# Trainium2, one core: the first pass of an encoder trunk with c from columns, chunk scales on ScalarE and the first query strip in another bank

## The chip, the core and the metric

The kernel runs on one core of one Trainium2 chip. The core has TensorE (PE in the profile, its weight loads PEld), VectorE (DVE), ScalarE (ACT), GpSimd (POOL) and SyncE (SP), which issues nearly all DMA transfers. Each engine works through its own instruction queue in order; semaphores let one wait for another. The metric is the device time of one execution in microseconds; less is better.

## What is computed

Two layers on 1024 tokens of width 1024 in float32, each with an RMS norm, a shift, scale and gate from a conditioning vector c, a token mixer, a SiLU gate and an output projection. Layer 0 is differential attention, layer 1 latent attention. The change touches only the start of layer 0:

```python
def _modulation(c, ada_w, ada_b):
    mod = jax.nn.silu(c) @ ada_w + ada_b
    shift, scale, gate = jnp.split(mod[:, None, :], 3, axis=-1)
    return shift, scale, gate
...
    for i in range(DEPTH):
        shift, scale, gate = _modulation(c, ada_w[i], ada_b[i])
        h = _rmsnorm(x, norm_g[i]) * (1.0 + scale) + shift
...
    proj = h @ w_in
    q, k, v, z = jnp.split(proj, [DA_WIDTH, 2 * DA_WIDTH, 3 * DA_WIDTH], axis=-1)
```

## The kernel before

All matrix products split a float32 operand into a high and a low part (names ending in h and l, or hi and lo) and add three products: high by high, high by low, low by high (`mm3`, lines 173 to 175). The high part is made by a cast on ACT, the low part by a subtraction on POOL or DVE.

**Start.** SP loads the small vectors (`vec`), the row of c (`crow`), four tiles of x (128 tokens x 1024), then the modulation weights. Line 561 issues warm-up matmuls on a tile of ones, 8 before the spread of c and 9 behind it (`WARM`). Lines 600 and 601 form silu(c) times two on one partition (the half stands in the dot's scale), and line 605 spreads it over all 128 partitions with a one-row matmul into `cb`, a PSUM tile of two banks. Tokens are scaled by their inverse RMS in two pieces: the first 256 columns (`X_CUT`) on ACT (lines 618 and 621), the other 768 on DVE (line 624, `x_rest`).

**First pass, tokens 0 to 511** (the loop from line 661 on). It runs over eight chunks k of 128 features. For each, SP loads two modulation weight tiles (`ada`, 512 KB each, four buffers) and a tile of value weights (`wvr`, 256 KB, two buffers). `mod_pair` does two dots of the ada tiles with cb on DVE (line 439) for shift and scale, and line 447 turns the scale into (1 + scale) times the norm's gain, one column, on DVE. `h_chunk` transposes four blocks of x on PE (line 487) and applies scale and shift on ACT twice, once rounded (h0h, line 492) and once in full (line 494); POOL subtracts (h0l, line 497). Then PE adds the chunk to four value accumulators (`vacc`) and one of a key strip (`kacc`): 15 matmuls of 512 columns on lines 712 to 718. Between the chunks DVE reduces the angles of the rotary tables (lines 580 to 595), ACT takes their sines (lines 633 to 636) and copies cb to SBUF (`c2`, line 637), for the modulation of layer 1.

**Behind it.** PE computes the first query strip (`qacc`, 24 matmuls) in a bank of the tag acc, which it shares with the value accumulators. ACT and DVE empty the accumulators into `v_hl` (lines 377 and 378), square and scale the other four x tiles (lines 530 to 532 and 732 to 733), and the **second half**, tokens 512 to 1023, goes through the same chunks, every second one transposed into the first bank of cb (tile `trc`). Four dots for layer 1 (`MODS_K`, from `mods_g`) stand between its chunks. Strips for key, query and gate follow, then the values of the other heads and the attention.

**What sets the order.** Instructions are issued by priority as their operands become ready in a schedule made at build time; `tc.issue_after(x)` keeps an instruction behind x. On the chip every queue then runs in that fixed order. A buffer is loaded again once its last reader is done, and `bank("acc", ...)` deals out five banks in turn.

Of the kernel before, what the change touches and what calls it, by code (L numbers as in the profile page):

```python
# [21 lines left out]
P = 128  # L22
# [10 lines left out]
      ("ada_bsc1", KT), ("subln_g", 1), ("q_a_norm_g", 3), ("kv_a_norm_g", 2), ("inv", 1), ("ada_bg0", KT), ("ada_bg1", KT)]  # L33
# [30 lines left out]
WARM = (8, 9)  # L64
# [17 lines left out]
def trunk(ctx: ExitStack, tc: tile.TileContext, A, out):  # L82
# [292 lines left out]
    def store_v(l, sp, acc, tt, fh, tag="vst", bufs=None):  # L375
        v = sp.tile([P, 2, HF], F32R, name="v_hl", tag=tag, bufs=bufs or VB[l])
        store_v.act = S.copy(v[:, 0, :], acc).ins
        V.tensor_sub(v[:, 1, :], acc, f32v(v[:, 0, :]))
# [62 lines left out]
    def mod_pair(l, j, ws, c_):  # L441

        g, bsh, bsc, a_, b_ = mods[l]
        js = slice(j, j + 1)
        mod_dot(ws[0], bsh[:, js], b_[:, js], c_)
        mod_dot(ws[1], bsc[:, js], a_[:, js], c_)
        return V.scalar_tensor_tensor(out=a_[:, js], in0=a_[:, js], scalar=1.0, in1=g[:, js], op0=ALU.add, op1=ALU.mult).ins
# [30 lines left out]
    def h_chunk(l, xn4, k, dst, hp, sub=G, wide=False, act=False, f32=None):  # L478

        _, _, _, a_, b_ = mods[l]  # L480
        if wide:
            tr = bank("cb", "trc", [P, D])[:, :HF].rearrange("p (j q) -> p j q", j=4)
        else:
            tr = bank("tr", "trh", [P, 4, P])
        for j in range(len(xn4)):
            nk = KT // len(xn4[j])
            PE.transpose(tr[:, j, :], xn4[j][k // nk][:, (k % nk) * P : (k % nk + 1) * P], ident)
# [7 lines left out]
        else:  # L495
            V.tensor_scalar(tmp, tr[:, :n, :], ak, bk, op0=ALU.mult, op1=ALU.add)
# [52 lines left out]
    def split_wv(raw, eng=G):  # L549
        h_ = p1b.tile([P, HF], F32R, name="wvh", tag="wv", bufs=16)  # L550
        l_ = p1b.tile([P, HF], F32R, name="wvl", tag="wv", bufs=16)
        S.copy(h_, raw)
# [10 lines left out]
    crow = p1.tile([P, D], F32, name="crow", tag="ada", bufs=ADA_B)  # L563
    th = p1.tile([P, D], F32, name="cth", tag="ada", bufs=ADA_B)
    SP.dma_start(crow[0:1, :], A["c"])
# [44 lines left out]
    y0 = [None] * 4  # L610
# [4 lines left out]
    y_ = inv_rms(ss0[:, 0:3], 3)  # L615
    for j in range(3):
        y0[j] = y_[:, j : j + 1]
        S.mul(xs0[j][0][:, :X_CUT], xs0[j][0][:, :X_CUT], y0[j])
    sq_halves([xs0[3][0][:, :HF], xs0[3][0][:, HF:]], ss0[:, 3:4])
    y0[3] = inv_rms(ss0[:, 3:4], 1)[:, 0:1]  # L620
# [1884 lines left out]
```

## Time and profile before

| | us |
|---|---|
| median of three runs | 1381.55 (1379.77 to 1382.26) |
| the profiled execution, whole | 1382.89 |
| its span | 1380.9 |

| page, share of the span busy | PE | PEld | DVE | ACT | POOL |
|---|---|---|---|---|---|
| | 99% | 83% | 69% | 53% | 51% |

The profile times each instruction of one execution. A row of the timeline has the start and length in us, engine, line, operation and the tiles (out<-in); in square brackets stands how long the engine sat idle before it and what ended that. A row of a window has its limits, then busy time and number of instructions of PE, PEld, DVE, ACT and POOL, the clock granted to TensorE (1.00 is full), the busy share of the DMA engines and the GB/s moved. A group has its count, busy time, mean length in ns, and idle time before it. In this program the span's first 57 us hold the first pass and the query strip.

### The profile page before, as it was taken

What the parts mean: (1) busy time and instruction counts of PE and PEld (TensorE: products, weight loads), DVE (VectorE), ACT (ScalarE), POOL (GpSimd) and SP (SyncE); (2) the same over time, 40 slices, a digit from 0 to 9 for tenths busy, and PEclk for the clock granted to TensorE, in tenths of its full rate; (3) what the DMA queues carried; (4) which work ended last, traced back from release to release, by engine and by line L of the source; (5) the groups of instructions that cost most, each with busy time, mean ns of one, the idle gap of its engine ahead of it and who ended that gap; (6) DMA issues with size and microseconds to landing.
All of it is one profiled execution on the core that took longest, in us unless ns stands there. A gap on an engine that the chain in (4) does not pass through costs nothing.

```text
span 1380.9 us, 20717 instructions
## 1 busy us (share of the span) xinstructions
PE 1361.0 (99%) x7322; PEld 1144.8 (83%) x7322; DVE 949.2 (69%) x1334; ACT 738.3 (53%) x1357; POOL 708.7 (51%) x556
## 2 busy tenths in 40 slices
PE   8999999999999999999999999999999999999997
PEld 6788888888888888887887887788888888888886
DVE  7764788877777767778597987645566555555584
ACT  5633465565655656566648543345454454455554
POOL 4425163647585757565695135532141373834673
PEclk8999999999999999999999999999999999999999
DMA  9867644353444444526654255599343463576373
GB/s 335 275 177 222 211 108 143 113 146 103 156 114 149 135 122 130 153 71 204 210 202 170 60 160 183 161 284 286 115 117 111 111 214 123 190 222 229 118 264 122
DMA packets 149386, 232.06 MB, mean 168 GB/s; under 512 B 20641, under 2 KB 57633, under 8 KB 149282
## 3 DMA queue, kind: packets, MB, share of 16 engines
q1 hardware_dynamic: 149138, 230.48, 53.4%
q8 instruction: 57, 0.93, 0.3%
q14 instruction: 47, 0.39, 0.1%
q10 hardware_dynamic: 144, 0.26, 0.1%
HBM read 144.74 MB, written 61.81 MB: 150 GB/s over the span
## 4 chain that ended last, share of the span: by engine, by line
PE 88%; DVE 4%; DMA 2%; ACT 2%; issue 1%; POOL 1%; SPq 0%; POOLq 0%; DVEq 0%; ACTq 0%
PE s L2109 10%; PE acc L173 9%; PE acc L175 9%; PE acc L174 9%; PE tr L398 8%; PE s L869 8%; PE pv L173 4%; PE pv L174 4%; PE pv L175 4%; PE oy L173 2%; PE oy L174 2%; PE oy L175 2%; PE vps L173 2%; PE vps L174 2%; PE vps L175 2%; PE zacc L175 1%
## 5 line engine op out<-in xcount | busy, mean ns | idle before, releaser
L400 ACT CAST pth<-tr 128x512 fp32r<-128x512 f32 x256 | 150.2, 587 | 279.2 <-PE tr L398 276.3
L401 DVE TENSOR_TENSOR ptl<-tr,pth 128x512 fp32r<-128x512 f32 x256 | 176.3, 689 | 144.6 <-ACT pth L400 143.9
L415 DVE TENSOR_REDUCE nm<-s 128x1 f32<-128x1024 f32 x192 | 234.0, 1219 | 53.7 <-PE s L869 42.9
L219 POOL TENSOR_TENSOR wl<-wraw,wh 128x512 fp32r<-128x512 f32 (+2 forms) x73 | 93.4, 1280 | 264.4 <-ACT wh L218 185.8
L417 ACT ACTIVATE e<-s,nm 128x1024 f32<-128x1024 f32 x128 | 143.7, 1122 | 35.0 <-DVE nm L415 34.4
L398 PE MATMUL tr<-ident,e 128*128 128x128 f32 x1024 | 154.8, 273 | 1.8 <-DVE ptl L401 1.5
L398 PEld LDWEIGHTS tr<-ident,e 128*128 128x128 f32 x1024 | 121.3, 140 | 42.5 <-DVE ptl L401 19.7
L173 PE MATMUL acc<-h0h,wh 128*128 128x512 f32 x360 | 149.5, 415 | 0.0
L173 PE MATMUL pv<-pth,vt 128*128 128x256 f32 x512 | 147.6, 288 | 0.0
L174 PE MATMUL pv<-ptl,vt 128*128 128x256 f32 x512 | 145.4, 284 | 0.0
L175 PE MATMUL pv<-pth,vt 128*128 128x256 f32 x512 | 144.6, 282 | 0.0
L175 PE MATMUL acc<-h0h,wl 128*128 128x512 f32 x360 | 142.0, 394 | 0.0
L174 PE MATMUL acc<-h0l,wh 128*128 128x512 f32 x360 | 141.4, 393 | 0.0
L174 PEld LDWEIGHTS pv<-ptl,vt 128*128 128x128 f32 x512 | 97.5, 190 | 2.5
L1203 POOL TENSOR_TENSOR wol<-wol,woh 128x512 fp32r<-128x512 f32 x56 | 81.9, 1486 | 34.0 <-ACT woh L1202 31.8
L173 PEld LDWEIGHTS pv<-pth,vt 128*128 128x128 f32 x512 | 97.2, 190 | 2.5
L175 PEld LDWEIGHTS pv<-pth,vt 128*128 128x128 f32 x512 | 97.4, 190 | 0.0
L869 PE MATMUL s<-ks,qa 128*128 128x512 f32 x256 | 82.7, 402 | 1.3 <-DVE e L877 1.2
L877 DVE SCALAR_TENSOR_TENSOR e<-s,z,e 128x1024 f32<-128x1024 f32 x64 | 82.2, 1284 | 2.2
L175 PEld LDWEIGHTS acc<-h0h,wl 128*128 128x128 f32 x360 | 67.6, 188 | 14.7
L869 PE MATMUL s<-ks,qb 128*128 128x512 f32 x256 | 79.6, 392 | 0.0
L174 PEld LDWEIGHTS acc<-h0l,wh 128*128 128x128 f32 x360 | 68.2, 189 | 9.2
(433 smaller groups left out, 3416.8 us busy)
## 6 DMA issues: line engine op xcount, KB each, us to landing
ada<-in_ada_ss SPq DMA_DIRECT2D x32, 512.0 KB, 6.1
vS<-v_hl SPq DMA_DIRECT2D x32, 512.0 KB, 5.5
vt<-vS SPq DMA_DIRECT2D x32, 512.0 KB, 4.6
wraw<-in_w_s SPq DMA_DIRECT2D x60, 256.0 KB, 2.8
wol<-tS SPq DMA_DIRECT2D x56, 256.0 KB, 5.3
tS<-ob SPq DMA_DIRECT2D x48, 256.0 KB, 2.2
rp_sw<-rp_raw SPq DMA_DIRECT2D x160, 64.0 KB, 2.0
bc_s<-bc_d SPq DMA_DIRECT2D x34, 256.0 KB, 4.0
```

The lines of the kernel that those rows point to most:

```text
L173: PE.matmul(psum, ah, bh, start=first, stop=False, skip_group_check=skip)
L174: PE.matmul(psum, ah, bl, start=False, stop=False, skip_group_check=skip)
L175: mm3.last = PE.matmul(psum, al, bh, start=False, stop=last, skip_group_check=skip).ins
L219: sub = (V if pair_of else G).tensor_sub(l_[:, :n], raw[:, :n], f32v(h_[:, :n]))
L398: transpose_p.last = PE.transpose(tr[:, j, :], p[:, kt * P : (kt + 1) * P], ident).ins
L400: mk["S"] = S.copy(pth[kh][:, :, dst], tr).ins
L401: mk["V"] = V.tensor_sub(ptl[kh][:, :, dst], tr, f32v(pth[kh][:, :, dst])).ins
L415: mk["V"] = V.reduce_max(nm, s_ps, axis=AX.X, negate=True).ins
L417: mk["S"] = S.activation(e, s_ps, AF.Exp, bias=nm, scale=1.0, accum_out=zs).ins
L869: PE.matmul(s_ps[:, kc * HF : (kc + 1) * HF], src[:, c, ql], KS[h][kc][:, c, :], start=fst, stop=not fst)
L877: combined.append(V.scalar_tensor_tensor(out=e0, in0=e1, scalar=z1[:, 0:1], in1=e0, op0=ALU.mult, op1=ALU.add).ins)
L2109: PE.matmul(s_ps[:, kc * HF : (kc + 1) * HF], lhs, rhs(kc), start=i == 0, stop=i == 4)
```

## The change

- **c from eight columns.** The row `crow` is no longer loaded; c arrives inside `vec` as eight columns of 128. Tanh and product work on 128x8. For each column, DVE multiplies the identity matrix by it (`cd`), and a matmul with ones spreads that block of 128 over all partitions: eight matmuls of 128 columns and 128 rows instead of two of 512 columns and one row. `cd` takes one of the four ada buffers; `crow` and `cth` took two.
- **Chunk scales.** Line 447's product leaves DVE; `mod_scale` does it on ACT just ahead of the chunk.
- **Token scaling.** `x_rest` of tiles 0 and 1 stays on DVE but stands one step later; tiles 2 and 3 go to ACT, behind the casts and the first chunks.
- **TensorE.** 15 instead of 9 warm-up matmuls behind the spread, and three more (`KEEP0`) into kacc behind the first chunk's transposes.
- **Query strip.** `qacc` lies in the second bank of the cb tile (`cbq`); the odd chunks of the second half use its first bank. The copy of cb to `c2` and the split of the query weights move behind the last chunk.
- **Order behind the first pass.** The squares of the second half's x come ahead of emptying the accumulators, its last two tiles are scaled between them, the four dots of layer 1 come behind its last chunk, and some later loads and splits wait for other instructions.

```diff
@@ _W @@
-      ("ada_bsc1", KT), ("subln_g", 1), ("q_a_norm_g", 3), ("kv_a_norm_g", 2), ("inv", 1), ("ada_bg0", KT), ("ada_bg1", KT)]
+      ("ada_bsc1", KT), ("subln_g", 1), ("q_a_norm_g", 3), ("kv_a_norm_g", 2), ("c", KT), ("inv", 1), ("ada_bg0", KT), ("ada_bg1", KT)]
-WARM = (8, 9)
+WARM = (8, 15)
+KEEP0 = 3
@@ strip_half @@
-    def strip_half(w, rhs, half):
+    def strip_half(w, rhs, half, acc=None):
-        acc = bank("acc", "acc")
+        acc = bank("acc", "acc") if acc is None else acc
@@ mod_pair @@
-        g, bsh, bsc, a_, b_ = mods[l]
+        _, bsh, bsc, a_, b_ = mods[l]
         js = slice(j, j + 1)
         mod_dot(ws[0], bsh[:, js], b_[:, js], c_)
-        mod_dot(ws[1], bsc[:, js], a_[:, js], c_)
-        return V.scalar_tensor_tensor(out=a_[:, js], in0=a_[:, js], scalar=1.0, in1=g[:, js], op0=ALU.add, op1=ALU.mult).ins
+        return mod_dot(ws[1], bsc[:, js], a_[:, js], c_).ins
+
+    def mod_scale(l, j):
+
+        g, _, _, a_, _ = mods[l]
+        js = slice(j, j + 1)
+        S.activation(a_[:, js], a_[:, js], AF.Identity, bias=g[:, js], scale=g[:, js])
@@ h_chunk @@
-        if wide:
-            tr = bank("cb", "trc", [P, D])[:, :HF].rearrange("p (j q) -> p j q", j=4)
+        if wide is not None:
+            tr = wide[:, :HF].rearrange("p (j q) -> p j q", j=4)
@@ the spread of c @@
-    crow = p1.tile([P, D], F32, name="crow", tag="ada", bufs=ADA_B)
-    th = p1.tile([P, D], F32, name="cth", tag="ada", bufs=ADA_B)
-    SP.dma_start(crow[0:1, :], A["c"])
+    cd = p1.tile([P, KT, P], F32, name="cd", tag="ada", bufs=ADA_B)
+    th, cs = [sm.tile([P, KT], F32, name="cth") for _ in range(2)]
...
-    c_act = S.activation(th[0:1, :], crow[0:1, :], AF.Tanh, scale=0.5).ins
-    c_last = V.scalar_tensor_tensor(out=crow[0:1, :], in0=th[0:1, :], scalar=1.0, in1=crow[0:1, :], op0=ALU.add, op1=ALU.mult).ins
+    c_act = S.activation(th, part("c"), AF.Tanh, scale=0.5).ins
+    V.scalar_tensor_tensor(out=cs, in0=th, scalar=1.0, in1=part("c"), op0=ALU.add, op1=ALU.mult)
     cb = bank("cb", "cb", [P, D])
-    for f in range(2):
-        fs = slice(f * HF, f * HF + HF)
-        spread = PE.matmul(cb[:, fs], ones[0:1, :], crow[0:1, fs], start=True, stop=True).ins
+    for k in range(KT):
+        c_last = V.tensor_scalar(cd[:, k, :], ident, cs[:, k : k + 1], None, op0=ALU.mult).ins
+        spread = PE.matmul(cb[:, k * P : k * P + P], ones, cd[:, k, :], start=True, stop=True).ins
@@ x_rest @@
-        V.tensor_scalar(xs0[j][0][:, X_CUT:], xs0[j][0][:, X_CUT:], y0[j], None, op0=ALU.mult)
+        rest = xs0[j][0][:, X_CUT:]
+        if j < 2:
+            V.tensor_scalar(rest, rest, y0[j], None, op0=ALU.mult)
+        else:
+            S.mul(rest, rest, y0[j])
@@ sines @@
-                S.copy(c2, cb)
@@ the first pass @@
-        if k < 0:
+        if k == 0:
             with tc.issue_after(m_last):
                 x_rest(0)
                 x_rest(1)
-        if k == 0:
-            with tc.issue_after(m_last):
-                x_rest(2)
-                x_rest(3)
...
-            with tc.issue_after(h_chunk.act):
-                wq0 = split_strip(qraw, None, ada_pair)
-            q_split = load_strip.last
         if 0 <= k < KT:
+            mod_scale(0, k)
             h_chunk(0, xs0, k, h0[k][0], p1, act=True)
+            if k == 0:
+                with tc.issue_after(h_chunk.tr):
+                    for _ in range(KEEP0):
+                        PE.matmul(kacc[:, 0:P], ones, ones, start=True, stop=True)
...
+            if k < 2:
+                with tc.issue_after(h_chunk.act if k else split_wv.act):
+                    x_rest(2 + k)
@@ behind the first pass @@
+    with tc.issue_after(h_chunk.act):
+        S.copy(c2, cb)
+        wq0 = split_strip(qraw, None, ada_pair)
...
-    qacc = strip_half(wq0, h0, 0)
+    cbq = bank("cb", "cbq", [P, D])
+    qacc = strip_half(wq0, h0, 0, cbq[:, HF:])
     q_mm = mm3.last
+    turn += 1
     for tt in range(4):
-        store_v(0, p1b, vacc[tt], tt, 0)
+        with tc.issue_after(x_last):
+            store_v(0, *((p1b, vacc[tt], tt, 0) if tt < 3 else (p1, vacc[tt], tt, 0, "xt", 6)))
+        if tt == 1:
+            yb = inv_rms(ssb, 2)
+            for j in range(2):
+                with tc.issue_after(store_v.v):
+                    V.tensor_scalar(xs1[2 + j][0], xs1[2 + j][0], yb[:, j : j + 1], None, op0=ALU.mult)
+                with tc.issue_after(store_v.act):
+                    S.mul(xs1[2 + j][1], xs1[2 + j][1], yb[:, j : j + 1])
...
-            if 0 < k <= MODS_K:
-                next(mods_g)
-            with tc.issue_after(q_split), tc.issue_after(q_mm):
-                h_last = h_chunk(0, xs1, k, h0[k][1], p1, V if k in HL_V else G, k % 2 == 1)
+            with tc.issue_after(store_v.act), tc.issue_after(q_mm):
+                h_last = h_chunk(0, xs1, k, h0[k][1], p1, V if k in HL_V else G, cbq if k % 2 else None)
+        if k == KT:
+            with tc.issue_after(h_chunk.v):
+                for _ in range(MODS_K):
+                    next(mods_g)
@@ the second value weights @@
-    wv1 = [load_wv(A["w_v0"][k, 1], V) for k in range(WV1)]
+    with tc.issue_after(h_chunk.act):
+        wv1 = [load_wv(A["w_v0"][k, 1], V) for k in range(2)]
```

The order of the instructions on three engines shows where they stand now. A row has line, operation, tile written <- tiles read, and shape; the lines are those of each kernel's own file.

SP, the first loads, in the kernel before (`wvr` and `wraw` are the first value and key weights, `posi` the positions):

```order
L148 DMA vec<-in_vec 128x71
L565 DMA crow<-in_c 1x1024
L523 DMA xt<-in_x 128x1024 x4
L434 DMA ada<-in_ada_ss 128x1024 x2
L543 DMA wvr<-in_w_v 128x512
L197 DMA wraw<-in_w_s 128x512
L543 DMA wvr<-in_w_v 128x512
L434 DMA ada<-in_ada_ss 128x1024
L669 DMA posi<-in_pos 128x256
L434 DMA ada<-in_ada_ss 128x1024 x3
```

SP, the same loads in the changed kernel:

```order
L149 DMA vec<-in_vec 128x79
L530 DMA xt<-in_x 128x1024 x4
L435 DMA ada<-in_ada_ss 128x1024 x2
L550 DMA wvr<-in_w_v 128x512
L198 DMA wraw<-in_w_s 128x512
L435 DMA ada<-in_ada_ss 128x1024 x2
L550 DMA wvr<-in_w_v 128x512
L677 DMA posi<-in_pos 128x256
L435 DMA ada<-in_ada_ss 128x1024 x2
```

The row of c is gone, and both ada tiles of step 1 stand ahead of the second value weights and the positions.

ACT, chunks 0 and 1 of the first pass, in the kernel before:

```order
L552 CAST wvh<-wvr 128x512
L492 ACTIVATE h0h_0_114<-trh,modb_103,moda_102 128x512
L494 ACTIVATE h_267<-trh,modb_103,moda_102 128x512
L218 CAST wh<-wraw 128x512
L552 CAST wvh<-wvr 128x512
L492 ACTIVATE h0h_0_118<-trh,modb_103,moda_102 128x512
L494 ACTIVATE h_295<-trh,modb_103,moda_102 128x512
```

ACT, the same chunks in the changed kernel:

```order
L559 CAST wvh<-wvr 128x512
L453 ACTIVATE moda_102<-moda_102,vec 128x1
L499 ACTIVATE h0h_0_114<-trh,modb_103,moda_102 128x512
L501 ACTIVATE h_284<-trh,modb_103,moda_102 128x512
L219 CAST wh<-wraw 128x512
L559 CAST wvh<-wvr 128x512
L633 ACTIVATE xt<-xt,rq_y 128x768
L453 ACTIVATE moda_102<-moda_102,vec 128x1
L499 ACTIVATE h0h_0_118<-trh,modb_103,moda_102 128x512
L501 ACTIVATE h_316<-trh,modb_103,moda_102 128x512
L633 ACTIVATE xt<-xt,rq_y 128x768
```

Each chunk has a one-column scale ahead of it, and the two token scalings of 768 columns stand among the first chunks.

ACT, from the end of the first pass to the second half, in the kernel before:

```order
L377 CAST v_hl<-vacc 128x512
L530 ACTIVATE junk,xss<-xth 128x512
L377 CAST v_hl<-vacc 128x512
L530 ACTIVATE junk,xs_589<-xth 128x512
L377 CAST v_hl<-vacc 128x512
L530 ACTIVATE junk,xss<-xth 128x512
L331 COPY rp_raw<-kacc 128x512
L530 ACTIVATE junk,xs_595<-xth 128x512
L733 ACTIVATE xth<-xth,rq_y 128x512 x2
L377 CAST v_hl<-vacc 128x512
L492 ACTIVATE h0h_1_116<-trh,modb_103,moda_102 128x512
```

ACT, the same place in the changed kernel:

```order
L332 COPY rp_raw<-kacc 128x512
L537 ACTIVATE junk,xss<-xth 128x512
L537 ACTIVATE junk,xs_612<-xth 128x512
L537 ACTIVATE junk,xss<-xth 128x512
L537 ACTIVATE junk,xs_618<-xth 128x512
L378 CAST v_hl<-vacc 128x512 x2
L757 ACTIVATE xth<-xth,rq_y 128x512 x2
L378 CAST v_hl<-vacc 128x512 x2
L499 ACTIVATE h0h_1_116<-trh,modb_103,moda_102 128x512
```

The copy of kacc, which reads the last sum of the first pass, stands first; the four squares follow together, and the accumulators are emptied two and two around the scaling of x.

More of the change, by code (lines that the diff above doesn't have):

```diff
@@ L377, in store_v @@
         store_v.act = S.copy(v[:, 0, :], acc).ins
-        V.tensor_sub(v[:, 1, :], acc, f32v(v[:, 0, :]))
+        store_v.v = V.tensor_sub(v[:, 1, :], acc, f32v(v[:, 0, :])).ins
         th, tl = tt // 4, tt % 4
@@ L486, in h_chunk @@
             nk = KT // len(xn4[j])
-            PE.transpose(tr[:, j, :], xn4[j][k // nk][:, (k % nk) * P : (k % nk + 1) * P], ident)
+            piece = xn4[j][k // nk][:, (k % nk) * P : (k % nk + 1) * P]
+            h_chunk.tr = PE.transpose(tr[:, j, :], piece, ident).ins
         n = len(xn4)
@@ L551, in split_wv @@
         l_ = p1b.tile([P, HF], F32R, name="wvl", tag="wv", bufs=16)
-        S.copy(h_, raw)
+        split_wv.act = S.copy(h_, raw).ins
         split_wv.last = eng.tensor_sub(l_, raw, f32v(h_)).ins
@@ L822, in trunk @@
     with tc.issue_after(store_v.act):
-        wv1 += [load_wv(A["w_v0"][k, 1], V) for k in range(WV1, KT)]
+        wv1 += [load_wv(A["w_v0"][k, 1], V) for k in range(2, KT)]
     with tc.issue_after(h_last):
@@ L827, in trunk @@
         pass
-    wz0 = split_strip(z0raw)
+    with tc.issue_after(store_v.act):
+        wz0 = split_strip(z0raw)
     q_done(0)(qacc, 0)
```

20 lines of the change are left out of this document (9 added, 11 removed).

## The prediction

> **What bounds the kernel now.** I read the page first, then the windows over the stretch that the change touches, the PE waits in it, and the timeline at each wait.
>
> ```profile
> PE 1361.0 (99%) x7322; PEld 1144.8 (83%) x7322; DVE 949.2 (69%) x1334; ACT 738.3 (53%) x1357; POOL 708.7 (51%) x556
> PE 88%; DVE 4%; DMA 2%; ACT 2%; issue 1%; POOL 1%; SPq 0%; POOLq 0%; DVEq 0%; ACTq 0%
> 14.94:21.53 6.59, 6.59 (x19) 5.30 (x20) 6.43 (x12) 3.28 (x6) 4.54 (x5) 0.54 1.01 374
> 21.53:49.35 27.82, 27.71 (x131) 21.83 (x129) 26.63 (x44) 17.33 (x28) 17.87 (x14) 1.00 0.92 321
> 49.35:57.24 7.89, 6.62 (x33) 5.36 (x33) 5.33 (x13) 6.28 (x16) 1.42 (x2) 1.00 0.79 202
> 57.24:81.70 24.46, 24.46 (x119) 20.29 (x120) 14.65 (x21) 7.79 (x12) 8.67 (x6) 1.00 0.66 206
> 81.70:100.00 18.30, 18.06 (x80) 14.61 (x80) 9.32 (x14) 6.82 (x12) 4.24 (x3) 1.00 0.78 224
> ```
>
> PE is the bound: 99% busy, 88% of the chain of waits. The orders of the two kernels run together again within the first tenth of the program, so the change is worth the time by which PE gets ahead before that. The window rows (us, then busy time and count of PE, PEld, DVE, ACT, POOL, then PEclk, DMA share, GB/s) show where it can. In step k=0 (14.94 to 21.53) PE is busy throughout, but at clock 0.54. In steps 1 to 7 it is busy 27.71 of 27.82 us, DVE 26.63: two engines near their limit. From the last matmul of step 7 (E = 49.35) to the first of the second token half (57.24) PE idles 1.27 us, later only 0.24.
>
> **Start of the first step.**
>
> ```profile
> 1.18 0.33 SPq L565 DMA_DIRECT2D crow<-in_c  x1
> 1.56 1.78 SPq L523 DMA_DIRECT2D xt<-in_x  x4
> 6.93 3.83 PE L561 MATMUL warm<-ones 128*128 128x128 f32 x18
> 11.29 1.28 DVE L439 CUSTOM_DVE_ANT_0 ada<-ada,cb,vec 128x1024 f32<-128x1024 f32 x1 [0.24 <-DMA ada<-in_ada_ss]
> 13.85 0.16 DVE L447 SCALAR_TENSOR_TENSOR moda<-moda,vec 128x1 f32<-128x1 f32 x1
> 14.11 0.78 ACT L492 ACTIVATE h0h<-trh,modb,moda 128x512 fp32r<-128x512 f32 x1 [0.23 <-DVE moda L447]
> 14.94 0.80 PE L712 MATMUL vacc<-wvh,h0h 128*128 128x512 f32 x1 [1.18 <-ACT h0h L492]
> L952 ACT ACTIVATE sl_w<-zz 128x4 f32<-128x4 f32 x7 | 1.4, 206 | 0.2
> ```
>
> The first dot waits for its load, and the loads leave SP one issue sooner without the row of c: 1.56 - 1.18 = 0.38. The new path of c is longer on DVE and PE (eight products; sixteen passes, which at 3.83 / 18 = 0.213 are 3.4 us), but the loads of x cover it, and nothing asks for cb before 10.9: cost nothing; without that cover, up to the 3.4. The scale (0.16 on DVE) becomes an ACT instruction like L952, 0.2. First matmul: 14.94 - 0.36 = 14.58.
>
> **Steps 0 to 2.**
>
> ```profile
> 9.93 7.53 DMA ada<-in_ada_ss
> 17.49 1.28 DVE L439 CUSTOM_DVE_ANT_0 ada<-ada,cb,vec 128x1024 f32<-128x1024 f32 x1
> 18.51 1.27 POOL L553 TENSOR_TENSOR wvl<-wvr,wvh 128x512 fp32r<-128x512 f32 x1
> 18.81 0.99 DVE L447 SCALAR_TENSOR_TENSOR moda<-moda,vec 128x1 f32<-128x1 f32 x1
> 19.89 0.78 ACT L492 ACTIVATE h0h<-trh,modb,moda 128x512 fp32r<-128x512 f32 x1 [3.31 <-DVE moda L447]
> 21.76 0.39 PE L712 MATMUL vacc<-wvh,h0h 128*128 128x512 f32 x1
> 25.64 0.39 PE L712 MATMUL vacc<-wvh,h0h 128*128 128x512 f32 x1
> L447 DVE SCALAR_TENSOR_TENSOR moda<-moda,vec 128x1 f32<-128x1 f32 x8 | 4.1, 507 | 0.3
> L624 DVE TENSOR_SCALAR xt<-xt,rq_y x4: 607/609/1708, 13.9 to 20.7; 128x768 f32<-128x768 f32 x4
> 16.00:17.00 1.00, 1.00 (x5) 0.80 (x4) 1.00 (x2) 0.58 (x2) 1.00 (x1) 0.50 1.03 410
> ```
>
> The one-column scale took 0.16 us alone and 0.99 beside POOL's subtraction, with which it ends at 19.8. Eight of them are 4.1 us of DVE; they leave. What is late next is the load of step 1's second dot. It landed at 9.93 + 7.53 = 17.46. The queue was full (share 1.03, 410 GB/s), so a load's place in it sets its time: this one now stands ahead of a weight tile and the positions (0.39 MB, 1.0 us) and starts 0.38 sooner: 16.05, its dot done at 17.4 (before 18.8). The weight tile follows it, 0.26 MB or 0.6 us: 16.7, its cast on ACT (0.6) done at 17.3. Then ACT has the token scaling of x2 (768 columns; 512 take 0.67 in the row of 54.20 below; I take 0.85), the scale 0.2, h0h 0.8: PE could start step 1 at 19.2. Its second matmul also needs wvl, 1.27 us of POOL after the cast, and DVE's token scalings (0.61 free, 1.71 beside POOL) compete with that: done between 18.6 and 20.4. I take 19.9 as step 1's start, against 21.76. A faster clock in step 0 gives nothing beyond that: a step at full clock takes 25.64 - 21.76 = 3.88, so step 0 would end at 18.5.
>
> Step 2: after 17.4 DVE does two token scalings (0.61 each), a cast and an angle of a third of their width (0.3 each, an estimate), a wait for POOL between 0 and 1.27 (I take 0.7) and two dots (2.6): 22.6. The scale 0.2 and the way over h0h to PE (14.94 - 14.11 = 0.83, and 0.2 before it) give 23.9; PE has ended step 1 at 23.8. Before 25.64: gain 1.7.
>
> **Steps 3 to 7.** DVE had 26.63 / 7 = 3.8 us a step; without L447 3.3. The loads are 1.31 MB a step, 3.2 us at 410 GB/s. Both are below PE's 3.88, so PE sets the pace and keeps its lead. The sine tables stay in their place, and with them two short waits:
>
> ```profile
> 34.02 1.28 ACT L633 ACT_TABLE_LOAD   x1
> 36.19 0.19 PEld L715 LDWEIGHTS kacc<-h0h,wl 128*128 128x128 f32 x1 [0.33 <-POOL wl L219]
> 37.95 0.42 PEld L487 LDWEIGHTS trh<-ident,xt 128*128 128x128 f32 x4 [0.54 <-ACT h L494]
> ```
>
> E falls at 47.65: gain 1.7. Bounds: 0.6 (steps 0 and 1 PE-bound at the old clock, rival 2) to 3.7 (PE without a gap from 14.58: 8 x 3.88 = 31.0, E = 45.6). I take 1.7, to which the DVE and POOL rows lead.
>
> **From E to the second half.**
>
> ```profile
> 50.19 0.50 PE L173 MATMUL acc<-h0h,wq 128*128 128x512 f32 x1 [0.84 <-DVE v_hl L378]
> 51.77 0.59 ACT L331 COPY rp_raw<-kacc 128x512 f32<-128x512 f32 x1
> 52.24 0.65 ACT L530 ACTIVATE junk<-xth 128x512 bf16<-128x512 f32 x1
> 52.77 0.21 ACT L530 ACTIVATION_READ_ACCUMULATOR junk<-xth 128x1 f32 x1
> 54.20 1.34 ACT L733 ACTIVATE xth<-xth,rq_y 128x512 f32<-128x512 f32 x2 [1.21 <-POOL rq_y L169]
> 55.45 0.56 ACT L377 CAST v_hl<-vacc 128x512 fp32r<-128x512 f32 x1
> 56.41 0.78 ACT L492 ACTIVATE h0h<-trh,modb,moda 128x512 fp32r<-128x512 f32 x1 [0.40 <-PE trh L487]
> 57.24 0.50 PE L173 MATMUL vacc<-wvh,h0h 128*128 128x512 f32 x1 [0.43 <-ACT h0h L492]
> ```
>
> The query strip waited 0.84 us for a bank to be emptied; in the second bank of cb it waits only for the copy of cb, two times 512 columns or at most 1.34 us, which ACT does while PE is in step 7. The 0.84 is not gained whole, since ACT is late next. Behind the copy of kacc, which now stands first and waits for E, it has four squares, four v_hl and two scalings of x. From start to start: 0.47, then 4 x 0.62, then the root (54.20 - 52.98 = 1.22, beside two v_hl), 1.25, and two v_hl of 0.5: h0h at E + 6.5, the matmul 0.83 later at E + 7.3 instead of E + 7.89. PE has its strip and transposes done at E + 6.6 (its 6.62 busy us). Gain 0.6; bounds -1.8 (ACT without any overlap, E + 9.7) and 1.27 (no idle time left). I take 0.6, since the rows show the overlap.
>
> **After that.**
>
> ```profile
> PE acc L173 <- DVE v_hl L378: 1.1, 2, 0.8
> ```
>
> Of this 1.1, 0.84 is counted; the other 0.24 is the idle time of the last window. The strip there no longer takes a bank that is being emptied: gain 0.24. The four dots of layer 1 move behind the second half's chunks, where DVE is busy 14.65 of 24.46 us. SP now waits for the first of them before the next weight tiles; the 18.3 us of strips in the last window hide that. Cost nothing; without that cover, one load's time.
>
> **Sum.** 1.7 + 0.6 + 0.24 = 2.5 us. The profiled execution took 1382.89 (span 1380.9 and 2.0 around it): 1380.4. It lies 1.34 over the median of 1381.55, and step 0 is one place where it may have been unlucky: at full clock step 1 could have begun at 20.7 (19.89 + 0.83) instead of 21.76. I give 0.3 of the 2.5 to that: 1381.55 - 2.2 = **1379.3 us**.
>
> **Rivals.**
> 1. *PE never waits in steps 1 and 2* (chance 0.25). DVE's scalings and POOL's subtractions miss each other, and the clock is full at 14.58. For it: 4.1 us leave a DVE that had 26.63 of 27.82. Against it: the weight tile that lands later. E gains its bound, 3.7, with 0.84 behind it: 1377.0.
> 2. *The clock stays half: keeping TensorE warm does not do what it says* (0.2).
>
> ```profile
> 10.00:11.00 1.00, 0.77 (x4) 0.47 (x3) 0.93 (x5) 0.68 (x2) 0.24 (x1) 0.61 1.01 412
> 14.00:15.00 1.00, 0.06 (x1) 0.07 (x1) 1.00 (x2) 0.89 (x2) 1.00 (x1) 0.60 1.07 398
> 21.00:22.00 1.00, 1.00 (x6) 0.76 (x5) 1.00 (x2) 0.85 (x2) 0.58 (x1) 0.99 0.84 324
> ```
>
> The mixed means put the clock's changes near 10.8, 14.2 and 21.0: steps of 3.4 us, or twice that. Up to 10.8 PE was busy with warm-up matmuls, and full clock followed; then it did four transposes up to 14.2, and half clock followed, even past 17.6. Now 62 passes run without a gap from about 1; at 0.213 us, and half of that once warm, they end between 9 and 11, and only transposes and six more passes come before 14.58. So the same low stretch may stand ahead of the first step. Step 0 then ends at 21.53 - 0.36 = 21.2 and step 1 at 25.05, 0.6 sooner than before; with 0.6 and 0.24, 1.4: 1380.2. [...]
> 3. *ACT's queue after E* (0.08), the slower case. If its instructions do not overlap, the matmul comes at E + 9.7, PE idles 3.1 us, about one such stretch, and half clock over the 6.8 us from 14.2 to 21.0 costs 3.4 more: 1.7 + 0.24 - 1.8 - 3.4 = 3.3 slower, 1384.8. [...]
>
> **Chances and range.** Forecast 0.47, rivals 0.25, 0.2, 0.08. About 0.2% (2.8 us) is what a measurement of this kernel can tell from no change: up to 1378.8 counts as faster. That takes rival 1 and a third of the forecast: 0.4 faster, 0.54 within, 0.06 slower. The forecast's own range is 1377.8 to 1380.8. The range of 8 in 10 takes in rivals 1 and 2 and the bounds of the terms, and leaves rival 3 out: 1376.3 to 1381.7.
>
> **What would show it.** First matmul at 14.6; the scale as 0.2 us on ACT, no L447 on DVE; step 1 from about 19.9 and step 2 from 23.9; PEclk back at 1.0 by 17.6; no wait before the query strip; E near 47.6; the second half from 55.0; no PE wait near 80. I am wrong if step 2 starts after 25, if PE idles over 2 us behind the query strip with a lower clock after it, or if PE waits for weight tiles near 100 us.

## Result and profile after

The changed kernel took **1388.85 us** (median of six runs, 1387.75 to 1391.49) against 1381.13 for the kernel before in the same series: ratio 1.0059, 95% interval 1.0046 to 1.0072. It is slower by about 8 us; I had forecast 1379.3. The profiled execution took 1388.8, its span 1387.0.

The page's row of busy times and the chain of work that ended last:

```profile
PE 1365.6 (98%) x7352; PEld 1146.0 (83%) x7352; DVE 943.7 (68%) x1332; ACT 742.4 (54%) x1367; POOL 710.3 (51%) x556
PE 86%; DMA 3%; DVE 3%; issue 2%; ACT 2%; POOL 2%; SPq 1%; POOLq 0%; DVEq 0%; ACTq 0%
```

PE is still the bound. It is busy 4.6 us longer, though the change added only small products at the start, in time that was mostly idle. That was the first hint that the loss was no wait.

The windows after, at the places of the five of before (columns as there):

```profile
14.94:21.53 6.59, 6.10 (x30) 4.45 (x30) 6.59 (x9) 5.34 (x9) 5.67 (x5) 1.00 1.05 405
21.53:50.20 28.67, 26.62 (x121) 21.57 (x120) 23.16 (x37) 18.13 (x31) 17.47 (x13) 0.94 0.93 318
50.20:58.09 7.89, 6.73 (x34) 5.21 (x32) 5.43 (x14) 7.37 (x17) 1.42 (x2) 1.00 0.86 221
58.09:82.50 24.41, 24.41 (x119) 20.27 (x120) 14.50 (x21) 7.92 (x12) 8.66 (x6) 1.00 0.57 181
82.50:100.00 17.50, 17.50 (x78) 14.30 (x78) 7.99 (x13) 6.83 (x12) 3.37 (x3) 1.00 0.76 229
```

Step 0 now has the full clock (1.00, before 0.54), and DVE is relieved (23.16 us, before 26.63). PE nevertheless is idle 2.05 us in the second row, and its clock there is 0.94. The timeline names the place:

```profile
14.63 0.49 PE L721 MATMUL vacc<-wvh,h0h 128*128 128x512 f32 x1 [0.64 <-ACT h0h L499]
18.01 0.38 ACT L453 ACTIVATE moda<-moda,vec 128x1 f32<-128x1 f32 x1
18.21 1.38 DVE L586 CAST ang<-posi 128x256 f32<-128x256 int32 x1
19.42 0.40 PE L721 MATMUL vacc<-wvh,h0h 128*128 128x512 f32 x1
20.04 1.38 DVE L587 TENSOR_SCALAR ang<-ang,vec 128x256 f32<-128x256 f32 x1
21.33 1.27 DVE L440 CUSTOM_DVE_ANT_0 ada<-ada,cb,vec 128x1024 f32<-128x1024 f32 x1
23.85 0.39 ACT L453 ACTIVATE moda<-moda,vec 128x1 f32<-128x1 f32 x1 [2.65 <-DVE moda L440]
24.95 0.77 ACT L501 ACTIVATE h<-trh,modb,moda 128x512 f32<-128x512 f32 x1
25.77 0.66 PE L494 MATMUL trh<-ident,xt 128*128 128x128 f32 x4 [2.05 <-ACT h L501]
26.18 0.52 PE L721 MATMUL vacc<-wvh,h0h 128*128 128x512 f32 x1
```

Step 1 starts early, at 19.42. Then two angle instructions of 256 columns take 1.38 us each beside POOL's subtractions, where I had 0.3; the dots of step 2 start at 21.33 only; and PE's queue has the transposes for the chunk after next ahead of step 2's first matmul, and they wait until `h` (24.95) has emptied the one bank for transposes. Step 2 starts at 26.18.

To see where the rest comes from I took the start of each matmul after, less the start of the same matmul before (**lag**, us, by the time before):

| | 57 | 132 | 140 | 168 | 380 | 640 | 1370 |
|---|---|---|---|---|---|---|---|
| after | 0.85 | 0.47 | 2.92 | 2.27 | 3.19 | 5.18 | 6.24 |

Less than one of the 6.2 us lies in the stretch that the change rewrote. (One profile stands for each kernel, and single executions scatter by a microsecond and more, so small differences of lags prove little.) The step at 136 is one wait:

```profile
131.46 1.28 DVE L440 CUSTOM_DVE_ANT_0 ada<-ada,c,vec 128x1024 f32<-128x1024 f32 x1 [6.63 <-DMA ada<-in_ada_ss]
137.69 1.28 DVE L440 CUSTOM_DVE_ANT_0 ada<-ada,c,vec 128x1024 f32<-128x1024 f32 x1 [4.33 <-DMA ada<-in_ada_ss]
138.90 0.69 DVE L379 TENSOR_TENSOR v_hl<-vps,v_hl 128x512 fp32r<-128x512 f32 x1
```

```profile
PE vps L174 <- DVE v_hl L379: 2.1, 1, 2.1
```

(DVE's timeline, then PE's only listed wait between 60 and 170 us: in all, times, longest). The subtraction that frees PE's bank stands in DVE's queue behind a dot of layer 1, whose load is late. After 168 the lag grows without a long wait: differences below 30 ns from one matmul to the next add up to 4.6 us. Short waits, the longest near 546 and 614, add some more, and two places where the kernel before waited and this one does not (near 718 and 848) take some off.

### The profile page after: what moved, and what is told of

Same layout as the page of the kernel before. It is cut to its first block, busy times and chain, and to the rows that moved or that the text cites. A ratio compares the mean times of both kernels' runs of the same rounds, so it can differ in the third digit from the quotient of the medians.

```text
span 1387.0 us, 20799 instructions
## 1 busy us (share of the span) xinstructions
PE 1365.6 (98%) x7352; PEld 1146.0 (83%) x7352; DVE 943.7 (68%) x1332; ACT 742.4 (54%) x1367; POOL 710.3 (51%) x556
## 4 chain that ended last, share of the span: by engine, by line
PE 86%; DMA 3%; DVE 3%; issue 2%; ACT 2%; POOL 2%; SPq 1%; POOLq 0%; DVEq 0%; ACTq 0%
PE s L2133 10%; PE acc L174 9%; PE acc L176 9%; PE acc L175 9%; PE tr L399 8%; PE s L893 8%; PE pv L174 4%; PE pv L176 4%; PE pv L175 4%; PE oy L174 2%; PE oy L176 2%; PE oy L175 2%; DMA ada<-in_ada_ss 2%; PE oz L174 1%; PE oz L176 1%
## 5 line engine op out<-in xcount | busy, mean ns | idle before, releaser
L345 POOL TENSOR_TENSOR rp_sw<-rp_sw,sinT 128x512 f32<-128x512 f32 x40 | 54.7, 1367 | 50.4 <-DMA rp_sw<-rp_raw 48.2
```

## Experiments

"Moved by" is the number of bytes by which the large tiles of SBUF's left pools stand elsewhere than before. "PE +" counts TensorE instructions (matmuls and weight loads in the trace) above the kernel before. "Pace" is the mean distance from one matmul of 512 columns to the next between 200 and 640 us (about 1190 of them, distances of 216 to 245 ns). "Long issues" are SP's DMA issues over 0.9 us from 160 to 640 us. Ratios are to the kernel before, run in turns with each.

| run | moved by | PE + | pace, ns | long issues | ratio (95%) |
|---|---|---|---|---|---|
| before | 0 | 0 | 230.5 | 1 | 1 |
| after | 160 | 60 | 232.1 | 11 | 1.0059 (1.0046 to 1.0072) |
| a1_dots_back | 160 | 60 | 232.1 | 10 | 1.0053 (1.0035 to 1.0070) |
| a2_first_only | 160 | 59 | 232.1 | 9 | 1.0052 (1.0032 to 1.0073) |
| a3_scale_x_back | 160 | 60 | 232.1 | 8 | 1.0051 (1.0036 to 1.0066) |
| a4_second_only | 32 | 1 | 231.9 | 2 | 1.0011 (1.0002 to 1.0021) |
| b1_shift32 | 32 | 0 | 231.9 | 3 | 1.0013 (1.0003 to 1.0022) |
| b2_shift160 | 160 | 0 | 232.1 | 2 | 1.0028 (1.0017 to 1.0039) |
| b5_shift512 | 512 | 0 | 230.7 | 3 | 0.9998 (0.9988 to 1.0008) |
| a5_aligned | 128 | 60 | 232.6 | 10 | 1.0047 (1.0032 to 1.0062) |
| a6_aligned_dots | 128 | 60 | 232.6 | 10 | 1.0031 (1.0018 to 1.0044) |
| a7_second_aligned_dots | 0 | 1 | 230.4 | 3 | 0.9993 (0.9984 to 1.0003) |
| a8_same_place | 0 | 60 | 230.6 | 10 | 1.0023 (1.0013 to 1.0032) |
| a9_same_place_dots | 0 | 60 | 230.6 | 10 | 1.0024 (1.0014 to 1.0035) |
| a10_same_dots_scale_x | 0 | 60 | 230.7 | 13 | 1.0032 (1.0020 to 1.0045) |
| b3_pe60 | 0 | 60 | 230.6 | 9 | 1.0040 (1.0025 to 1.0056) |
| b4_pe256 | 0 | 257 | 230.5 | 3 | 1.0034 (1.0021 to 1.0048) |
| a11_same_count | 0 | 0 | 230.4 | 3 | 0.9999 (0.9990 to 1.0008) |
| a12_strip_only | 0 | 0 | 230.5 | 3 | 0.9986 (0.9977 to 0.9995) |
| a13_first_strip | 0 | -1 | 230.6 | 3 | 0.9989 (0.9980 to 0.9998) |

### First theory: the moved dots of layer 1

```diff
 a1: for k in range(KT + SKEW1): if k < KT:
+            if 0 < k <= MODS_K: next(mods_g)
-        if k == KT: ... for _ in range(MODS_K): next(mods_g)
 a2: from the copy of cb to c2 on, every line of before
 a3: mod_scale and x_rest as before (on DVE, at their old places)
 a4: c from one row, WARM = (8, 9), no KEEP0, mod_scale and x_rest as before; the rest as changed
```

> The changed kernel with one thing undone: the four dots of layer 1 stand between the chunks k = 1 to 4 of the second token half again. Theory A (the moved dots hold up SP's queue, everything later in the first 140 us arrives late, and the 2 us wait for v_hl at 136 us and the slow loss after 164 us both come from that): no such wait, the second half near 1382, at most 1 us above the kernel before. Theory B (only the 2.4 us near 136 come from the dots, the slow loss of 3 us in the attention has another cause): about 1386. Theory C (the dots have nothing to do with it): 1388.8.

> Only the first pass of the change (columns of c, scale on ScalarE, token scalings, warm-up); from the copy of cb on, everything as in the kernel before. By the trace the first pass loses 0.3 to 0.9 us by the end of step 7. Theory A (all that is lost later comes from the second part): 1381.5 to 1382. Rival (the first pass moves the queues so that the later waits come in any case): 1385 or more.

> The changed kernel with the scale back on VectorE and the token scalings back on VectorE at their old places; columns of c, warm-up and the whole second part as changed. Theory D (the stall at 25.8 us comes from the scalings and angle instructions that now stand ahead of the dots of step 2): step 2 starts by 25.0 and stays at full clock, the lag at 57 us falls from +0.85 to about -0.5, the time by about 1.3 to 1387.5 if the late waits stay. Rival (the transposes of k = 3 that now stand ahead of step 2 make the stall): step 2 still starts after 26, 1388.8.

> Only the second part of the change (query strip in the second bank, squares ahead of v_hl, dots and loads moved); c from one row, warm-up and the first pass as before. Theory A: wait for v_hl near 136 us as in the changed kernel, and the slow loss: 1387.5 to 1388.5. Rival (the late waits need the first pass's lag): below 1385.

Theory A falls. With the dots back nearly everything is still lost, 1388.57; the first pass alone, which was to cost 0.9, loses as much, 1389.44; the second part alone, which by theory A was to take 1387.5 to 1388.5, takes 1383.39 (its profiled run was its slowest, 1386.82). In a3 the stall at 25.8 us is gone, with one of 1.16 at 20.3 in its place: the lag at 57 us is -1.02, further down than theory D had it (-0.5), but the time stays. So the loss sits in what a1, a2 and a3 share and a4 has not, and it takes effect hundreds of microseconds later, where the order of instructions is the same in all of them. They share the columns of c and the warm-up. The pace column shows something that even a4 has: matmuls at 232 instead of 230.5 ns. What a4 shares is the longer `vec`, which moves every tile allocated behind it.

### Second theory: the place of the tiles in SBUF

The left pools begin behind `const`, `sm` and a pad (`PADL`, 96 bytes). The eight columns lengthen `vec` by 32 bytes, and the two tiles `cth` take 4 x 32 in `sm`: 160.

```diff
 b1: -PADL = 96 // 4   +PADL = 128 // 4      (before, else unchanged)
 a5: -PADL = 96 // 4   +PADL = 64 // 4       (after); a6: and the dots back
 a7: a4 with the dots back and PADL = 64 // 4: the old addresses
```

> The kernel before with one number changed: the pad of the left side of SBUF is 32 bytes longer, so that the tiles of the left pools start at 32 over a multiple of 128 bytes, as they do in the changed kernel, instead of at multiples of 128. Nothing is computed otherwise. Theory L (the slow loss of the attention is the place of the tiles: the longer vec and the tiles of c moved everything by 160 bytes): matmuls of 512 columns from 230.5 to 232 ns, 4 to 5 us more, 1386.5. Rival R (the loss comes from the warm-up or from the clock of the start): no change, 1382.5.

> The changed kernel with the pad 32 bytes shorter, so that the left tiles start at multiples of 128 bytes again. Theory L: the slow loss of 3 to 5 us goes, the first pass and the wait for v_hl stay: 1384 to 1385. Rival R: 1388.7.

> As the last one, and the four dots of layer 1 between the chunks again. Theory L with the moved dots as the second cause: lag at 132 us about -1.3, wait for v_hl at most 1.1, no slow loss: 1381.5 to 1383, the time of before. Rival R: 1388.5.

> Only the second part of the change (first pass as before), with the dots between the chunks and the tiles at the addresses of the kernel before. Its sibling at 32 over, with the dots moved, was 2.5 us ahead of the kernel before at 132 us and lost 4.9 at the wait for v_hl. If the dots make that wait and the address the rest: 1380.5, some 2 us under the kernel before. Rival (the wait for v_hl comes from the loads that the second part moved, not from the dots): 1383.

Half right. b1 has the slower pace and is slower than before, but by 1.8 us, not 4 to 5. a5 and a6 miss (1387.89 and 1386.71): at a multiple of 128 the pace is even worse, 232.6. a7, at exactly the old addresses, has the old pace, 230.4, and takes 1381.30. So the multiple of 128 was the wrong rule. b2 puts the tiles of the kernel before where the change has them; a8, a9 and a10 put the changed kernel's back.

```diff
 b2: -PADL = 96 // 4   +PADL = 256 // 4      (before, else unchanged)
 a8: -th, cs = [sm.tile([P, KT], F32, name="cth") for _ in range(2)]
     +th, cs = mods[1][3:]                    and PADL = 64 // 4
 a9: a8 and the dots back;  a10: a9 and mod_scale, x_rest as before
```

> The kernel before with its left pad 160 bytes longer: every tile of the left pools at exactly the address that it has in the changed kernel, and nothing else touched. Theory L (the place of the tiles alone makes the slow loss and with it the short waits at 480 to 600 us, which every kernel with the columns of c shows): 1386 to 1387.5, matmuls of 512 columns at 232 ns to the end, lag 0 at 132 us and growing to 4 or 5. Rival (an address costs no more than the shift by 32 bytes did, 2 us; the rest comes from the first pass): 1384.4.

> The changed kernel with all large tiles at the addresses of the kernel before: the two small tiles of c lie in moda1 and modb1, the pad is 32 bytes shorter. Theory L: matmuls at 230.4 ns as before, no growing lag after 168 us; what is left is the first pass and the wait for v_hl: 1383.5 to 1385. Rival (waits at 480 to 600 us come from the first pass): 1386.5.

> As the last one, and the four dots of layer 1 between the chunks again. Theory L with the dots as second cause: lag -1.5 at 132 us and kept: 1381 to 1382, within 0.1% of the kernel before. Rival: 1384.5.

> As the last one, with the scale and the token scalings back on VectorE at their old places; of the first pass only the columns of c and the longer warm-up stay. If the scalings ahead of the dots of step 2 make the stall at 25.8 us: lag about -2.5 at 132 us, 1380 to 1381, some 2 us under the kernel before. Rival (the transposes of k = 3 ahead of step 2 make it): as the last one.

Both directions agree: the place alone costs 0.28%, some 3.9 us (b2), and taking it out of the change gains 0.36% (1.0059 to 1.0023 in a8). Two starts of the same two matmuls, with no wait of PE between them, before, in b2 and in a8:

```profile
200.55 0.62 PE L869 MATMUL s<-ks,qa 128*128 128x512 f32 x2
382.80 0.62 PE L869 MATMUL s<-ks,qa 128*128 128x512 f32 x2
```

```profile
203.21 0.63 PE L869 MATMUL s<-ks,qa 128*128 128x512 f32 x2
386.25 0.62 PE L869 MATMUL s<-ks,qa 128*128 128x512 f32 x2
```

```profile
201.26 0.62 PE L893 MATMUL s<-ks,qa 128*128 128x512 f32 x2
383.61 0.62 PE L893 MATMUL s<-ks,qa 128*128 128x512 f32 x2
```

The same work takes 182.25, 183.04 and 182.35 us. No list of waits shows this. Between 168 and 1370 us the differences below 30 ns from one matmul to the next add up to 4.6 us in b2, as in the changed kernel, and to 0.3 in a8. A last run asked which part of the address counts:

```diff
 b5: -PADL = 96 // 4   +PADL = 608 // 4      (before, else unchanged)
```

> The kernel before with its left pad 512 bytes longer: every left tile moves, but against the tiles of the right pools, which stay, it keeps its place within 512 bytes (left and right both start at 384 over a multiple of 512, as in the kernel before). Theory L1 (what counts is the place within 512 bytes, or of left against right tiles within 512): matmuls of 512 columns at 230.5 ns between 200 and 640 us, time as before, 1382.5. Theory L2 (any other place than the tuned one costs): 231.9 to 232.6 ns, 1384.3 to 1386.

L1: old pace, old time (1383.22 against 1383.23). In the kernel before, nearly all large tiles, left and right, start at 384 over a multiple of 512 bytes; a shift by 512 keeps that, shifts by 32, 128 and 160 don't. Whether the place itself counts or that of left against right was not tried, nor why it does. The wait for v_hl near 136 us does not go with the pace: b5, at the old pace, has one of 1.4 us there, as b2 has.

But a8, a9 and a10 are still 0.23 to 0.32% slower, with old addresses and, behind the first pass, the old order: the short waits behind 400 us stayed, and Theory L had explained too much. The dots made no difference (a9), and a10, 1.45 us ahead at 132 against 1.12 in a9, missed the 2.5.

### Third theory: where TensorE's instructions are fetched

In a8, SP's issue of one copy that PE needs took four times its usual length. Its timeline, the matmul that waited for that copy, and the transfers that started in the same 2.6 us:

```profile
407.61 0.54 SPq L373 DMA_DIRECT2D qb<-qb  x1
408.28 1.92 SPq L374 DMA_DIRECT2D qb<-qb  x1
411.48 0.70 PE L893 MATMUL s<-ks,qb 128*128 128x512 f32 x2 [0.62 <-DMA qb<-qb]
```

```profile
q1 hardware_dynamic: 224, 0.36, 61.2%
q8 instruction: 1, 0.02, 3.7%
```

and the same copies before, with the transfers of 405 to 409, among them no instructions:

```profile
407.14 0.51 SPq L372 DMA_DIRECT2D qb<-qb  x1
407.76 0.54 SPq L373 DMA_DIRECT2D qb<-qb  x1
```

```profile
q1 hardware_dynamic: 450, 0.68, 69.8%
```

The page of a8 lists queue q8 with 58 packets and 0.95 MB: packets of 16384 bytes, one every 24 us, and per packet 7352 x 2 / 58 = 254 of TensorE's matmuls and weight loads. From this count I take the packets to be TensorE's instructions; that is an estimate, which b3 and b4 below try, since they add instructions on TensorE alone. Between 160 and 640 us, over all twenty profiles, 114 of the 126 long issues overlap such a packet, and about 190 of the 6534 short ones. Outside that stretch only 215 of 733 long issues do, so there most have another cause. That such a packet delays a DMA issue is my reading of this overlap. By an estimate from these counts, sixty more instructions move every packet by 60 / 254 of 24 us, or 5.7 us, against the program. The traces show somewhat less: in the ten kernels with 59 or 60 more, the packets between 160 and 640 us come 3.5 to 4.1 us earlier in the program than before (the median of each kernel). In the other nine, among them b4 below with 257 more, the median moved by 0.1 us or less.

```diff
 b3: in before, behind keep_busy(WARM[1]):
+        for _ in range(15):
+            PE.matmul(warm[0:1, 0:1], ones[0:1, 0:1], ones[0:1, 0:1], start=True, stop=True)
 b4: as b3, range(64)
 a11: a8 with  -WARM = (8, 15)  +WARM = (8, 3)   -KEEP0 = 3  +KEEP0 = 0
```

> The kernel before, all tiles at their addresses, with 15 products of one element by one behind the warm-up: 60 more instructions on TensorE, as many as the change adds, and nearly no time. Theory F (TensorE's instructions come in packets of 16384 bytes about every 22 us; SP's DMA issues that fall together with such a packet take 1 to 2 us instead of 0.46; 60 instructions more move every packet by some 5 us against the program, onto copies that PE waits for): 8 to 11 issues over 0.9 us between 160 and 640 us instead of 1 to 2, short PE waits near 409, 487, 546 to 556 and 614 us, 2 to 3.5 us more: 1385. Rival W (the missing load of the row of c, or the first pass's order on SP, makes the long issues): 1 to 3 of them, 1382.4.

> The changed kernel with the tiles at the addresses of before, as a8, and with 12 warm-up products and the three keep-warm products less, so that TensorE has as many instructions ahead of the first step as the kernel before. Theory F: 1 to 4 issues over 0.9 us between 160 and 640 us, none of the waits from 409 us on: 1382 to 1383.5. Rival W: 10 of them, 1385.3 as a8.

> As b3, with 64 instead of 15 products of one element by one behind the warm-up: 256 instructions more, one whole packet of 16384 bytes. Theory F (what counts is where in the program the packets fall): they fall where they fell in the kernel before, so 1 to 4 issues over 0.9 us between 160 and 640 us, no waits from 409 us on, and only the time of the products themselves, up to 2 us behind the idle time of 1.5 us at the start, as a constant lag: 1383.5 to 1385. Rival (more instructions cost more, whatever their number): at least as many long issues and waits as b3, 1389 or more.

Theory F held in all three, on the long issues and on the waits. PE's waits between 405 and 620 us, in b3, then b4, then a11:

```profile
PE s L871 <- DVE e L879: 1.6, 2, 0.9
PE s L871 <- DMA qb<-qb: 0.2, 1, 0.2
```

```profile
PE s L871 <- DVE e L879: 0.4, 1, 0.4
```

```profile
PE s L893 <- DVE e L901: 0.4, 1, 0.4
```

The kernel before has 0.4 there too. b3 is 5.5 us slower, more than I expected, since a wait for v_hl at 136 us came on top (lag 0.82 at 132, 5.34 at 140): 2.6 us of idle time, and then 3.4 us at half clock. From 380 to 640 us its lag grows by 2.4, in b4 it falls by 0.2. b4 paid more at the start than expected: its lag is 3.3 at 57 us, with a wait of 2.53 at the query strip, and 4.1 from 100 on. Its profile ends 2.8 us behind, all of it from the start; the ratio, from four runs, says 4.7 us, and the rest stays unexplained. In the long part of the program b4 runs like the kernel before. And a11, the whole change without its addresses and without its sixty instructions, is no slower than before.

The two causes also show apart in the lag between 168 and 1370 us. Differences below 30 ns add up to 4.6 us where only the place differs (b2) and to 0.1 where only the count does (b3). Single steps of over 0.3 us add nothing in b2, 1.7 us in b3 and 3.8 in a8, which has the sixty instructions without the place.

### What of the change is worth keeping

```diff
 a12: a7, and wv1, wz0, lam as before (WV1 = 3, no lam_at)
 a13: a11, with the dots back and wv1, wz0, lam as before
```

> First pass, addresses, dots and the loads of the next weight tiles as in the kernel before; of the change are left the query strip in the second bank, the squares ahead of v_hl and the later split of the query weights. Its sibling with the loads moved was 2.0 us ahead at 132 us and lost 1.0 at the wait for v_hl. If the moved loads make that wait: ahead by 2 to the end, 1380, a ratio near 0.9985. Rival (PE's own lead makes it, since v_hl is bound by loads): 1381.3.

> The changed kernel with tiles and instruction count as in the kernel before (a11), and with the dots of layer 1 and the loads of the next weight tiles back at their old places: left are the columns of c, the scale on ScalarE, the token scalings, and the query strip in the second bank. a11 was 1.8 us ahead at 132 us and lost it at 152 us in a wait for e. If the moved dots and loads make that wait: ahead by 1.8 or more to the end, 1380.5 to 1381, a ratio near 0.9987. Rival (the wait comes with any lead): 1382.6.

Both come out slightly ahead of both kernels: 1380.83 and 1380.44 us, ratios 0.9986 and 0.9989, with intervals that end just below 1. Their profiles are ahead by 2.13 and 1.77 us at 132 us and lose 0.39 and 0.85 at the wait for v_hl. That wait I could not settle: from 100 to 150 us the profiles lose between nothing (b4, a11, and a5 and a6 with 0.2 or less) and 5.0 us (a4), with the dots moved (after, a4, a8) or not (a9, b2, b3), so it doesn't hang on the dots alone. In the four with the largest losses, 3.7 to 5.0 us (a3, a4, a10, b3), 3.4 us at half clock follow the wait.

## Why the prediction was wrong

**The step that failed** is the first one, "the orders of the two kernels run together again within the first tenth of the program, so the change is worth the time by which PE gets ahead before that." The orders do run together. The time doesn't: tile addresses and the places of the instruction packets stay changed to the end (in the profile after the packets still come 5.7 us earlier in the program from 640 us on, by the median). They cost 0.36% and 0.24% here (after to a8, a8 to a11), some 5.0 and 3.3 us, which is the whole loss; the second figure takes the warm-up with it. Neither is in my sum, and no rival of mine has a mechanism of the kind. The diff showed both: a longer `vec` and more matmuls.

The other steps, by the profile after:

- **First matmul** forecast 14.58, was 14.63. Right. The scale on ACT costs 0.38, not 0.2.
- **Clock.** Rival 2 did not come in the profile after: step 0 ran at full clock. In a11, without the longer warm-up and the three products, it ran at half clock. But so it did in a1, which has both, for 3.4 us, and in b2, with the warm-up of before, it had the full clock:

```profile
10.00:14.00 4.00, 2.56 (x16) 1.61 (x14) 3.05 (x9) 2.98 (x9) 1.85 (x3) 1.00 1.03 410
14.00:18.00 4.00, 2.88 (x14) 2.09 (x14) 3.33 (x5) 3.11 (x5) 3.47 (x4) 1.00 1.03 397
```

```profile
10.00:14.00 4.00, 1.53 (x4) 0.64 (x4) 2.53 (x5) 3.31 (x8) 2.19 (x3) 0.74 1.04 407
14.00:18.00 4.00, 3.95 (x11) 3.25 (x12) 3.92 (x6) 3.10 (x6) 3.46 (x4) 0.50 1.04 399
```

```profile
14.00:18.00 4.00, 3.60 (x11) 2.97 (x12) 3.54 (x6) 3.11 (x6) 3.47 (x4) 0.57 1.03 398
14.94:21.53 6.59, 5.55 (x23) 3.69 (x24) 6.39 (x11) 3.30 (x6) 4.96 (x5) 1.00 1.02 400
```

  (the windows of after, of a11, then one of a1 and one of b2; the clock is the third number from the end). Over all profiles, step 0 had the full clock throughout in 8 of the 9 with the longer warm-up and in 3 of the 11 without. So keeping TensorE warm seems to make the full clock likelier, but it neither ensures it nor is always needed. It was worth little: at 100 us a11 is 1.8 us ahead of the kernel before, and a8, with the full clock, 1.1.
- **Step 1** forecast 19.9, was 19.42. Right. So was the remark that the profile before was unlucky in step 0: in b2, b5 and a12, which have the old first pass and there the full clock, step 1 starts at 20.2 to 20.7, as the prediction had it, not at 21.76.
- **Step 2** forecast 23.9, was 26.18, against 25.64 before. Mis-sized was "a cast and an angle of a third of their width (0.3 each, an estimate)": 1.38 each beside POOL (0.28 and 0.34 in the kernel before, where they started at 19.7 and 20.5). Overlooked was that PE's queue has the next transposes ahead of this step. The rule that I had applied to the token scalings (0.61 free, 1.71 beside POOL) I did not apply to the short instructions.
- **Gain by E** forecast 1.7, was a loss of 0.9. The idle 2.05 us were followed by half clock:

```profile
26.00:30.00 4.00, 4.00 (x14) 3.18 (x13) 3.97 (x7) 2.21 (x5) 3.78 (x3) 0.57 0.91 297
```

  In a5 too (0.57), but in a2, a6, a8 and a9, with the same 2.0 to 2.1 us of idle time, the clock stayed at 1.00. There the lag at 57 us is -0.57 to -1.26, so the drop cost some 1.4 to 1.9 us (after against a8, a5 against a6). The changes of clock in each trace lie 3.41 us or a multiple of it apart. Counted on in such steps, the idle stretch lies whole within one step in after and a5, and is divided over two in the other four. Over all twenty profiles, from 21 to 1370 us, each of the six steps with over 2.0 us of idle time of PE was followed by half clock, and none of those with less than 1.7 us was; of two with 1.8 us, one was. Rival 3 reckoned with half clock behind 3.1 us of idle time; no run shows that as the length it takes, and in after and a5 2.0 to 2.1 us were followed by it.
- **From E to the second half** forecast 7.3, was 7.9, as before. Mis-sized were ACT's four squares: 0.76 each from start to start, not 0.62:

```profile
50.37 0.59 ACT L332 COPY rp_raw<-kacc 128x512 f32<-128x512 f32 x1 [2.71 <-PE kacc L727]
53.76 1.05 ACT L378 CAST v_hl<-vacc 128x512 fp32r<-128x512 f32 x2
57.25 0.79 ACT L499 ACTIVATE h0h<-trh,modb,moda 128x512 fp32r<-128x512 f32 x1
58.09 0.50 PE L174 MATMUL vacc<-wvh,h0h 128*128 128x512 f32 x1 [1.16 <-ACT h0h L499]
```

  The wait before the query strip is gone, as forecast, and ACT is late next. More was to be had: in a4, a7 and a12, which have the old first pass, two of the squares stand ahead of the copy of kacc. From the start of the last matmul of step 7 to that of the second half they take 7.1 to 7.3 us, against 8.28 before and 8.15 after. ACT in a12, where the copy waits 0.32 us instead of 2.71:

```profile
47.90 0.63 ACT L538 ACTIVATE junk<-xth 128x512 bf16<-128x512 f32 x1
48.95 0.59 ACT L332 COPY rp_raw<-kacc 128x512 f32<-128x512 f32 x1 [0.32 <-PE kacc L721]
```

- **After that**: the wait near 82 us went, as forecast. That the moved dots cost nothing, since "the 18.3 us of strips in the last window hide that", can't be upheld or refuted: a wait came at 136 us, but also in kernels that left the dots in place.

With addresses and instruction count restored and the dots and loads left alone (a13), the change gains 0.11% (0.02 to 0.20), 1.5 us against the forecast of 2.2. That the two are near is luck. a12, with the old first pass, gains as much as a13 (0.14%): by the profiles 0.4 us by E and 1.1 from there to the second half, where a13 gains 1.1 and 0.1. And the gain by E, forecast 1.7, is within the scatter of single profiles: the last matmul of step 7 starts at 48.5 us on the mean of the nine with the whole new order of the first pass (47.8 to 49.9), and at 48.7 on the mean of the seven with the old first pass (47.9 to 49.3). So that term is not shown.

## What to carry to other kernels

Before arguing from waits, list what an edit changes for the rest of the program: the bytes it adds ahead of other tiles (160 alone cost 0.28% here, b2), and the instructions it adds ahead of others on the longest queue (60 alone cost 0.40%, b3). If a kernel has a pad, set it again with every change of its small tiles, and run the old kernel with the new addresses alone and with the new instruction count alone as controls. Take more than one profile before a part of a microsecond is put down to an edit: b5, the old kernel at other addresses and with the old pace, reached the second half 1.2 us sooner than the profile before. A lag that grows in steps under 30 ns, as by 4.6 us in b2, stands in no list of waits: compare the time between two equal instructions far apart in both traces.

## What was not expected of the hardware

- Matmuls of 128x512 in this kernel start 230.4 to 230.7 ns apart with the left tiles at their old place or 512 bytes on, and 231.9 to 232.6 with them 32, 128 or 160 bytes on. The whole kernel was 0.13% (b1), 0.28% (b2) and 0.36% (after against a8) slower by it.
- Between 160 and 640 us, an SP DMA issue that overlaps a packet of TensorE's instructions takes 1 to 2.4 us instead of 0.46 in over a third of the cases (114 of about 305), and a copy that PE needs can come late by it (0.62 us of waiting in a8). Which issues are hit changes with the number of instructions ahead: in the kernels with 60 more there were 8 to 13 long issues between 160 and 640 us, with about 256 more 3 again, with none more 1 to 3.
- PE need not be idle for a whole step of 3.41 us to fall to half clock: over 2.0 us within one step was followed by it in six of six cases, 1.8 us in one of two, under 1.7 us in none (twenty profiles, 21 to 1370 us).
